# An earlier first product: one weight split traced behind two input tiles, and products of a zero tile during the first loads

## The chip, the cores and the metric

The kernel runs on one core of a Trainium2 chip. The metric is the device time of one execution in microseconds (us). The kernel before took 1235.92 us as the median of three runs (1230.69, 1235.92 and 2627.81 us).

## What is computed

Two layers of an encoder trunk over 512 tokens of width 1024, all in float32. Each layer normalises its input, projects it into the operands of an attention group (q, k, v) and of a bidirectional scan group (z, x/B/C, dt), joins both results in an output projection with a residual, and adds a gated feed-forward part. Cut to what matters here:

```python
for i in range(DEPTH):                      # DEPTH = 2
    h = rms_norm(x, norm_mix_w[i])
    proj = jnp.einsum("bld,de->ble", h, w_in[i])
    q, k, v, z, xbc_raw, dt_raw = jnp.split(proj, split_at, axis=-1)
    ...
    x = x + jnp.einsum("ble,ed->bld", mixed, w_out[i])
    h = rms_norm(x, norm_ffn_w[i])
    g = jnp.einsum("bld,df->blf", h, w_gate[i])
    u = jnp.einsum("bld,df->blf", h, w_up[i])
    x = x + jnp.einsum("blf,fd->bld", jax.nn.silu(g) * u, w_down[i])
return rms_norm(x, final_norm_w)
```

The change touches the first projection of layer 0 alone: the columns for k, v and dt (272 of them, "kvdt"), and what stands ahead of it.

## The kernel before

The activations are held transposed, as eight tiles x of 128 features by 512 tokens. Weights come in pieces of up to 1024 columns by 128 partitions. A product of two float32 operands is made from three products in TensorE's float32r format: each operand is split into a rounded high part and the rest, and high x high, high x low and low x high are added up in PSUM.

**Splitting.** W is a stream of weight pieces in a fixed order. W.split(j) (lines 180 to 195) takes piece j: ScalarE casts it to the high part whi (line 191), VectorE subtracts that from the raw piece and gives wlo (line 192). W.next() hands out the next piece and splits up to two ahead. Raw pieces lie in two buffers called wraw; a piece that is split frees its buffer, and the load of a later piece waits for that on the SP queue (line 177). The inputs are split in the same way: Norm.tile(k) casts x tile k times the norm's weights to xh on ScalarE (line 306) and computes xl on VectorE (line 307). Norm.square(k) squares a tile into one of two buffers sqt (line 319) and adds it to ssq (line 322).

**The start.** SP issues the loads of x tile 0, a small piece of the parameters (line 242), and x tiles 1 to 7 (line 240). ScalarE's queue issues pieces 0 and 1 of kvdt (piece 0 in two halves) and then pieces 2 and 3, which get a place of their own ("early"). The trace order is then: split of piece 0, split of piece 1, the eight tiles with the splits of pieces 2 and 3 among them, the squares.

**The first projection.** For each k-step (one x tile), four blocks of 128 tokens get three products of 272 columns each (lines 418 to 420), so 12 products a k-step and 96 in all. Piece 0 holds the weights of k-steps 0 and 1, piece 1 of 2 and 3, and so on. The results stay in four PSUM banks (two of tag "a", two of "s") until the norm's scale is known: the sum of squares is added over partitions by eight small products (line 328), VectorE computes the reciprocal root rtok (lines 284 to 290), and ScalarE scales the banks into kvd (line 464).

**What follows.** Attention (first product with V: line 717), the fill-in projections (q first, 256 columns each, lines 418 to 420 again; the x/B/C projections at lines 410 to 412) and the scan are traced as three generators in turns. The norm's scale is spread over tokens by a full float32 product with a tile of ones (line 343). The feed-forward part's first cast of summed operands is at line 1013.

**Order.** The program is traced in this order, and then a planner puts each engine's instructions in an order of its own, from a simulation of the timeline in which trace order gives the priority:

```python
with tile.TileContext(nc, schedule_with_timeline_sim=True) as tc:
```

So what is traced later can run earlier where its engine would be free. Each engine then executes its list strictly in the planned order.

Of the kernel before, what the change touches and what calls it, by code (L numbers as in the profile page):

```python
# [15 lines left out]
F32 = mybir.dt.float32  # L16
# [7 lines left out]
P = 128  # L24
# [17 lines left out]
OUTE, _, YE, HE, WE, RAE, MLE, DSE = "AVGVGVVG"  # L42
# [36 lines left out]
def tile_hybrid_encoder(ctx, tc, xt_d, par_d, rope_d, snw_d, w_kvdt, w_xbc, w_q, w_z, w_out, w_gate, w_up, w_down, out_d):  # L79
    nc = tc.nc  # L80
    V, A, G, T = nc.vector, nc.scalar, nc.gpsimd, nc.tensor
# [4 lines left out]
    nrm = ctx.enter_context(tc.tile_pool(name="nrm", bufs=1))  # L86
# [9 lines left out]
    def bank(tag):  # L96


        return psum.tile([P, S], F32, name=f"ps_{tag}", tag=tag)
# [107 lines left out]
    W = Stream()  # L207
# [49 lines left out]
    for name, op in (("lt", ALU.is_gt), ("le", ALU.is_ge)):  # L257
        m = const.tile([P, P], F32, name=f"m_{name}")
        G.affine_select(out=m, in_=ones, pattern=[[1, P]], compare_op=op, fill=0.0, base=0, channel_multiplier=-1)
        mask[name] = m  # L260
    for name, op in (("gt", ALU.is_gt), ("ge", ALU.is_ge)):
        m = const.tile([P, P], F32, name=f"m_{name}")
# [7 lines left out]
    inv = const.tile([P, 1], F32, name="inv")  # L270
    V.memset(inv, 1.0 / D)

    warm = const.tile([P, 1], F32, name="warm")
    A.activation(warm, inv, AF.Tanh)

# [160 lines left out]
    def mixer(l, norm, mx):  # L436
        op = norm.op
        if l == 0:
            early = mx.tile([P, 2, WU], F32, name="early", tag="qr")
            for j in (2, 3):  # L440
                W.raw[j] = early[:, j - 2]
                W.fetch(j, 0, chunks[j][1], A)
            W.split(0)
            W.split(1)
            for k in range(KT):
                norm.tile(k)
                if k in (3, 5):
                    W.split(k // 2 + 1)
            for k in range(KT):
                norm.square(k, V, V if k == 0 else None)  # L450
# [516 lines left out]
    for l in range(L):  # L967
        with tc.tile_pool(name=f"mx{l}", bufs=1) as mx:
            norm = mixer(l, norm, mx)
        with tc.tile_pool(name=f"ff{l}", bufs=1) as ff:  # L970
# [46 lines left out]
            for f in range(PLAIN):  # L1017
# [11 lines left out]
                if f == 0:  # L1029
                    with tc.high_priority():  # L1030
                        _, rb = norm.finish()
# [160 lines left out]
```

## Time and profile before

| | |
|---|---|
| median of three runs | 1235.92 us |
| the profiled execution's own time | 1231.69 us |
| its span in the trace | 1230.0 us |
| TensorE busy | 1198.6 us, 97% |
| VectorE busy | 902.4 us, 73% |
| ScalarE busy | 630.5 us, 51% |
| GpSimd busy | 157.8 us, 13% |
| first product on TensorE | 9.42 us |

PE is TensorE (PEld its weight loads), DVE VectorE, ACT ScalarE, POOL GpSimd, SP SyncE, whose queue issues most DMAs. L191 is line 191 of the kernel. A busy TensorE isn't necessarily one at its peak: the ends of its products are modelled, so the distance from one start to the next says more than a duration. Where a row merges several instructions (x2), its time runs from the first start to the last end, and neighbouring instructions of one engine overlap in the records by about 0.1 us.

### The profile page before, as it was taken

Reading aid. Unit: us, or ns where it says so; the run is one execution under the profiler, and the core shown is the slowest. Engines: PE = TensorE matmul, PEld = TensorE weight load, DVE = VectorE, ACT = ScalarE, POOL = GpSimd, SP = SyncE. Lnnn points to the kernel's source line nnn. Section 1 sums busy time; section 2 is a strip of 40 time slices with the busy share of each in tenths; the row PEclk is TensorE's granted clock in tenths of the full one; section 3 lists DMA queues with packets and bytes.
Section 4 is the critical chain, followed back from the end, with each engine's and each line's share of the span. In section 5 each row is a group of like instructions: output and inputs, shape, how many; then the busy total and the mean of one; then the engine's idle time right before and its main releaser. Section 6 shows DMA issues by size and latency. Waiting matters only on the chain.

```text
span 1230.0 us, 19740 instructions
## 1 busy us (share of the span) xinstructions
PE 1198.6 (97%) x7718; PEld 1059.6 (86%) x7718; DVE 902.4 (73%) x1475; ACT 630.5 (51%) x1203; POOL 157.8 (13%) x144
## 2 busy tenths in 40 slices
PE   6999999999999999999999999999999999999996
PEld 6788886687899899899898898777879989989985
DVE  6898976457887677677679977856698847847843
ACT  5678675244354254254465776744444623623544
POOL 0203433011100000000202144401020000000002
PEclk9999999999999999999999999999999999999998
DMA  6221212224243234231442111212243333333121
GB/s 224 73 73 48 66 37 68 69 69 142 89 126 120 65 120 126 64 104 39 126 147 91 69 35 61 87 35 69 77 146 112 105 110 95 102 114 95 35 72 75
DMA packets 47534, 110.04 MB, mean 89 GB/s; under 512 B 5425, under 2 KB 5937, under 8 KB 47441
## 3 DMA queue, kind: packets, MB, share of 16 engines
q1 hardware_dynamic: 46720, 107.68, 27.7%
q8 instruction: 60, 0.98, 0.3%
q10 hardware_dynamic: 720, 1.11, 0.3%
q14 instruction: 34, 0.27, 0.1%
HBM read 104.44 MB, written 4.33 MB: 88 GB/s over the span
## 4 chain that ended last, share of the span: by engine, by line
PE 86%; DVE 9%; ACT 2%; issue 1%; DMA 1%; POOL 0%; ACTq 0%; DVEq 0%; POOLq 0%
PE ps_a L1054 6%; PE ps_a L1053 6%; PE ps_a L1052 6%; PE ps_a L410 5%; PE ps_a L411 5%; PE ps_a L412 5%; PE ps_a L1099 3%; PE ps_a L1098 3%; PE ps_a L1100 3%; PE ps_s L1098 3%; PE ps_s L1099 3%; PE ps_s L1100 3%; PE ps_s L1054 3%; PE ps_s L1053 3%; PE ps_s L1052 3%; PE ps_t L717 3%
## 5 line engine op out<-in xcount | busy, mean ns | idle before, releaser
L191 ACT CAST whi<-wraw 128x512 fp32r<-128x512 f32 (+4 forms) x183 | 125.5, 714 | 217.7 <-PE ps_a L411 57.6
L191 ACT CAST whi<-sraw 128x1024 fp32r<-128x1024 f32 x126 | 131.6, 1050 | 141.2 <-DVE sraw L166 40.7
L192 DVE TENSOR_TENSOR wlo<-wraw,whi 128x512 fp32r<-128x512 f32 (+4 forms) x183 | 152.5, 845 | 59.5 <-ACT whi L191 58.4
L192 DVE TENSOR_TENSOR wlo<-sraw,whi 128x1024 fp32r<-128x1024 f32 x126 | 153.5, 1223 | 46.5 <-ACT whi L191 46.3
L410 PE MATMUL ps_a<-xh,whi 128*128 128x512 f32 x320 | 128.3, 405 | 5.5 <-ACT kvd L464 1.7
L411 PE MATMUL ps_a<-xl,whi 128*128 128x512 f32 x320 | 128.2, 402 | 0.0
L412 PE MATMUL ps_a<-xh,wlo 128*128 128x512 f32 x320 | 127.8, 399 | 0.0
L322 POOL TENSOR_TENSOR ssq<-ssq,sqt 128x512 f32<-128x512 f32 x17 | 25.2, 1481 | 671.1 <-ACT sqt L319 670.8
L166 DVE TENSOR_TENSOR sraw<-sraw 128x1024 f32<-128x1024 f32 x72 | 88.0, 1222 | 1.0
L418 PE MATMUL ps_a<-whi,xh 128*128 128x256 f32 (+1 forms) x256 | 74.6, 292 | 9.4 <-ACT xh L306 9.4
L1054 PE MATMUL ps_a<-ss,wlo 128*128 128x256 f32 x288 | 81.7, 284 | 0.0
L1052 PE MATMUL ps_a<-ss,whi 128*128 128x256 f32 x288 | 81.5, 283 | 0.0
L1053 PE MATMUL ps_a<-ss,whi 128*128 128x256 f32 x288 | 81.5, 283 | 0.0
L1054 PE MATMUL ps_a<-s,wlo 128*128 128x256 f32 x288 | 81.1, 283 | 0.0
L1053 PE MATMUL ps_a<-s,whi 128*128 128x256 f32 x288 | 81.1, 283 | 0.0
L410 PEld LDWEIGHTS ps_a<-xh,whi 128*128 128x128 f32 x320 | 61.6, 193 | 22.1 <-ACT s L1013 4.0
L1052 PE MATMUL ps_a<-s,whi 128*128 128x256 f32 x288 | 79.8, 283 | 0.0
L411 PEld LDWEIGHTS ps_a<-xl,whi 128*128 128x128 f32 x320 | 61.4, 192 | 15.5 <-DVE xl L94 1.5
L419 PE MATMUL ps_a<-wlo,xh 128*128 128x256 f32 (+1 forms) x256 | 74.2, 291 | 0.0
L412 PEld LDWEIGHTS ps_a<-xh,wlo 128*128 128x128 f32 x320 | 61.4, 192 | 14.7 <-issue 2.0
L420 PE MATMUL ps_a<-whi,xl 128*128 128x256 f32 (+1 forms) x256 | 72.5, 287 | 0.0
L1098 PE MATMUL ps_s<-hid,whi 128*128 128x512 f32 (+1 forms) x182 | 69.9, 384 | 0.0
(399 smaller groups left out, 3420.4 us busy)
## 6 DMA issues: line engine op xcount, KB each, us to landing
sraw<-in_w_gate SPq DMA_DIRECT2D x72, 256.0 KB, 5.6
sraw<-in_w_up SPq DMA_DIRECT2D x72, 256.0 KB, 4.2
wraw<-in_w_down SPq DMA_DIRECT2D x48, 384.0 KB, 3.5
wraw<-in_w_xbc SPq DMA_DIRECT2D x16, 512.0 KB, 3.3
wraw<-in_w_out SPq DMA_DIRECT2D x16, 512.0 KB, 4.2
wraw<-in_w_q SPq DMA_DIRECT2D x8, 512.0 KB, 3.3
wraw<-in_w_z SPq DMA_DIRECT2D x8, 512.0 KB, 3.4
wraw<-in_w_gate SPq DMA_DIRECT2D x8, 512.0 KB
```

What stands on the lines that cost most here:

```text
L166: V.tensor_tensor(q[to], q[to], q[by], ALU.add)
L191: A.copy(hi[:, u], raw[:, u])
L192: (G if lo_pool else V).tensor_tensor(lo[:, u], raw[:, u], hi[:, u].bitcast(F32), ALU.subtract)
L410: T.matmul(ps, lhsT=wh, rhs=op.h[k], start=first, stop=False)
L411: T.matmul(ps, lhsT=wh, rhs=op.l[k], start=False, stop=False)
L412: T.matmul(ps, lhsT=wl, rhs=op.h[k], start=False, stop=last)
L418: T.matmul(ps, lhsT=xh, rhs=wh, start=first, stop=False)
L419: T.matmul(ps, lhsT=xh, rhs=wl, start=False, stop=False)
L1052: T.matmul(out, lhsT=wh[:, o:o + P], rhs=x_[:, 0, i], start=first and i + j == 0, stop=False, skip_group_check=True)
L1053: T.matmul(out, lhsT=wh[:, o:o + P], rhs=x_[:, 1, i], start=False, stop=False, skip_group_check=True)
L1054: T.matmul(out, lhsT=wl[:, o:o + P], rhs=x_[:, 0, i], start=False, stop=i == 3, skip_group_check=True)
L1098: T.matmul(ps[:, cols], lhsT=w1[:, o:o + P], rhs=h, start=f == a, stop=False)
```

## The change

A tile of zeros, 128 x 256, is set on VectorE, in one of the two buffers of the squares (tag sqt), and five full float32 products of it with itself are written into a bank of tag "m" that nothing reads. They are traced ahead of everything else that TensorE does. The split of weight piece 1 is no longer traced directly behind that of piece 0, but behind the first two input tiles; the splits of pieces 2 and 3 stay behind tiles 3 and 5.

```diff
@@ -270,6 +270,12 @@
     inv = const.tile([P, 1], F32, name="inv")
     V.memset(inv, 1.0 / D)
 
+
+    idle = nrm.tile([P, 256], F32, name="idle", tag="sqt", bufs=2)
+    V.memset(idle, 0.0)
+    b = bank("m")
+    for _ in range(5):
+        T.matmul(b[:, :256], lhsT=idle[:, :P], rhs=idle, start=True, stop=True)
     warm = const.tile([P, 1], F32, name="warm")
     A.activation(warm, inv, AF.Tanh)
 
@@ -441,10 +447,9 @@
                 W.raw[j] = early[:, j - 2]
                 W.fetch(j, 0, chunks[j][1], A)
             W.split(0)
-            W.split(1)
             for k in range(KT):
                 norm.tile(k)
-                if k in (3, 5):
+                if k in (1, 3, 5):
                     W.split(k // 2 + 1)
             for k in range(KT):
                 norm.square(k, V, V if k == 0 else None)
```

## Rows read from the trace of the kernel before

**Rows 1.** The page, part 1: busy time (share), instructions of each engine.
```profile
PE 1198.6 (97%) x7718; PEld 1059.6 (86%) x7718; DVE 902.4 (73%) x1475; ACT 630.5 (51%) x1203; POOL 157.8 (13%) x144
```

**Rows 2.** Timeline, first 10 us: start, length (us), engine, line, operation [idle before].
```profile
1.72 6.70 SPq L240 DMA_DIRECT2D x<-in_xt  x7
...
3.94 0.69 DVE L315 TENSOR_TENSOR ssq<-x 128x512 f32<-128x512 f32 x1 [2.95 <-DMA x<-in_xt]
4.32 0.74 ACT L191 CAST whi<-wraw 128x272 fp32r<-128x272 f32 x2 [0.61 <-DMA wraw<-in_w_kvdt]
...
8.10 0.64 ACT L191 CAST whi<-wraw 128x544 fp32r<-128x544 f32 x1 [3.04 <-DMA wraw<-in_w_kvdt]
...
8.65 1.33 ACT L306 ACTIVATE xh<-x,par 128x512 fp32r<-128x512 f32 x2
8.78 0.73 DVE L192 TENSOR_TENSOR wlo<-wraw,whi 128x544 fp32r<-128x544 f32 x1 [3.22 <-ACT whi L191]
...
9.42 1.41 DVE L307 SCALAR_TENSOR_TENSOR xl<-x,par,xh 128x512 fp32r<-128x512 f32 x2
...
9.42 0.59 PE L418 MATMUL ps_a<-whi,xh 128*128 128x272 f32 x1 [9.42 <-ACT xh L306]
```

**Rows 3.** Windows, TensorE: from:to, length, busy (instructions), granted clock, DMA share, GB/s.
```profile
9.40:14.80 5.40, 5.38 (x24) 1.00 1.01 377
14.80:24.12 9.32, 9.32 (x74) 1.00 0.34 111
32.60:35.40 2.80, 2.80 (x7) 0.50 0.01 3
```

**Rows 4.** Windows, all engines in order PE, PEld, DVE, ACT, POOL; clock, DMA.
```profile
10.00:15.00 5.00, 5.00 (x24) 5.00 (x23) 5.00 (x9) 5.00 (x10) 0.00 (x0) 1.00 1.01 376
```

**Rows 5.** Timeline, 28 to 33 us: sum of squares, kvd, first product of line 410.
```profile
28.68 0.95 PE L328 MATMUL ps_m<-inv,ssq 128*128 128x1 f32 x8
...
32.05 0.87 ACT L464 ACTIVATE kvd<-ps_a,rtok 128x272 f32<-128x272 f32 x2 [4.45 <-DVE rtok L290]
...
32.59 0.80 PE L410 MATMUL ps_a<-xh,whi 128*128 128x512 f32 x1 [1.66 <-ACT kvd L464]
```

**Rows 6.** Windows, all engines, as rows 4: a stretch ahead of the attention.
```profile
75.00:100.00 25.00, 25.00 (x156) 21.43 (x155) 24.76 (x46) 19.86 (x45) 0.00 (x0) 1.00 0.20 64
```

**Rows 7.** Lines 464, 717, 1013 by layer: ns min/median/max, first and last start.
```profile
L464 ACT ACTIVATE kvd<-ps_a,rtok x2: 481/484/488, 32.0 to 32.4; 128x272 f32<-128x272 f32 x2
L464 ACT ACTIVATE kvd<-ps_a,rtok x2: 482/485/488, 633.0 to 633.4; 128x272 f32<-128x272 f32 x2
L717 PE MATMUL ps_t<-t_ring,Vt x256: 272/273/324, 95.3 to 230.6; 128*64 128x128 f32 x128
L717 PE MATMUL ps_t<-t_ring,Vt x256: 272/273/324, 696.3 to 829.8; 128*64 128x128 f32 x128
L1013 ACT CAST s<-xn x3: 1039/1044/1058, 293.0 to 296.6; 128x1024 fp32r<-128x1024 f32 x3
L1013 ACT CAST s<-xn x3: 1040/1045/1058, 890.6 to 894.2; 128x1024 fp32r<-128x1024 f32 x3
```

**Rows 8.** The first parameter piece (tile par): its DMA from issue to landing.
```profile
DMA to landing us min/median/max: 3.1/3.1/3.1
```

**Rows 9.** Timeline, 20 to 26 us: both q pieces and the last squares.
```profile
20.21 0.33 SPq L177 DMA_DIRECT2D wraw<-in_w_q  x1
...
21.71 1.29 DVE L192 TENSOR_TENSOR wlo<-wraw,whi 128x512 fp32r<-128x512 f32 x2
...
23.64 1.14 ACT L191 CAST whi<-wraw 128x512 fp32r<-128x512 f32 x2 [1.18 <-DMA wraw<-in_w_q]
...
24.90 0.69 DVE L322 TENSOR_TENSOR ssq<-ssq,sqt 128x512 f32<-128x512 f32 x1
25.50 0.69 DVE L192 TENSOR_TENSOR wlo<-wraw,whi 128x512 fp32r<-128x512 f32 x1
```

**Rows 10.** Line 343, full float32 products of both layers: ns min/median/max, starts.
```profile
L343 PE MATMUL ps_m<-dg,ones x8: 591/592/592, 38.4 to 884.9; 128*128 128x512 f32 x8
```

## The prediction

> **What bounds the kernel now.** I read the page first, then the order of instructions in the first 45 us, then busy time by stretch, then single lines in both layers.
>
> The page has TensorE busy for 97% of the span [rows 1], so only stretches in which it is idle, or runs slowly, can give anything. The start is such a stretch. The timeline shows why [rows 2]: ScalarE finishes the cast of weight piece 0 at 5.06 us, then stands idle 3.04 us until the DMA of piece 1 lands at 8.10. The first two input casts (xh, line 306) are queued behind that cast, although the first input tile was there at 3.94, when VectorE squared it. They run at 8.65, VectorE has nothing to do from 5.56 to 8.78 in consequence, and the first product starts at 9.42.
>
> From there TensorE is dense but slow at first: 24 products in the 5.40 us to 14.80, then 74 in 9.32 us [rows 3]. That is 0.225 and 0.126 us each; for 272 columns these are 1.2 and 2.4 GHz. (The clock column has 1.00 in both; I go by the spacing.) The reader should now look at the feeders: from 10 us VectorE and ScalarE are busy in all of the 5.00 us, and the DMA share is 1.01 [rows 4]. So the front has two limits close together, TensorE and the engines that split its operands.
>
> The next wait is at 30.9 us. A product of line 410 needs a bank that ScalarE empties with kvd (line 464), which waits 4.45 us for rtok; that chain of VectorE starts behind the sum of squares, line 328, at 28.68; line 410 starts at 32.59 [rows 5]. After it VectorE is the bound up to the attention: 24.76 busy of 25 us between 75 and 100 [rows 6]. The time from kvd to the first attention product of line 717 is the same in both layers, 63.3 us [rows 7]. So the number to forecast is how much earlier **kvd** starts.
>
> **The change, part by part.**
>
> *The moved split.* It consists of one cast on ScalarE and one subtraction on VectorE; piece 1's DMA is issued earlier in the program, and its place is not changed. But the buffer of piece 1 is released by the subtraction, and the load of a q weight waits on SP for that release. The cast can't start before 8.10 in either kernel, so if both input tiles are through by then, this costs nothing. New on ScalarE: input cast 0 at 5.06, cast 1 at about 5.7, both done near 6.4 (1.33 us for two [rows 2]); on VectorE two subtractions (1.41 us) in the hole from 5.56 to 8.78. The first product moves from 9.42 to about 5.06 + 0.77 = 5.83 us (0.77 is from the start of the first cast, 8.65, to the product, 9.42): 3.6 us earlier. Needed are the parameters, which land 3.1 us after an issue that precedes 1.72, so by 4.8 [rows 2, 8], and tile 1. Its landing is not shown: its issue is at 1.72 and the second cast ran unhindered behind the first, by 9.3, so it lies between 4.8 (3.1 us, as the parameters) and 9.3. I take 5 to 6, nearer to the parameters and to tile 0, which was issued just ahead of it and was there at 3.94.
>
> *What this is worth behind 8.1 us.* ScalarE's list from there is shorter by two casts, 1.33 us, VectorE's by 1.41 us. If a square (0.6 us) and its addition (0.69) also slip into the hole, it is up to 1.9 and 2.1; if tile 1 lands at 9.3, nothing. As both engines are full in this stretch, what they produce comes earlier by that much, not by 3.6. I take 1.4. What TensorE needs from them last is the second q piece: its DMA is issued at 20.21, behind the release of a buffer, lands at 23.64, and its last subtraction ends at 26.19; the sum of squares is complete at 24.90 + 0.69 = 25.59 [rows 9]. With 1.4 taken off these are 24.8 and 24.2.
>
> *The sum of squares.* In the kernel before, 2.5 us of q products lie on TensorE between the last subtraction (26.19) and line 328 (28.68). TensorE came late there; now it would not. If all of them depend on that last piece, line 328 comes at 24.8 + 2.5 = 27.3, a gain of 1.4; if none do, at about 24.8, a gain of 3.9; with 2.1 in place of 1.4, at most 4.6. Half of the products take weights that were there before, so I take the middle, **2.6 us**, and keep 1.4 and 4.6. kvd starts 3.4 us behind line 328 as now, at 29.4.
>
> *The zero products.* One set of zeros on VectorE, idle before 3.94, and five products of 256 columns in full float32. The nearest row is line 343, 512 columns: eight records for the four norms, so two a product, 0.591 us each [rows 10]. As upper bound at half the clock I take the same 0.591 for 256 columns: 5 x 2 x 0.591 = 5.9 us, from about 1.2 to 7.1, which would hold up the first product by 1.3; as lower bound half of it, over by 4.2. Either way line 328 isn't touched, since k-steps 0 and 1 have to be done only by 9.4, when piece 1 is split. The tile takes one of two buffers of the squares until then; the squares of the first tiles that need the second come later. Cost **0**, between 0 and 0.6 (one square that misses the hole).
>
> What the clock is worth: if the products raise it, the 24 slow ones save 24 x (0.225 - 0.126) = 2.4 us of TensorE. But without that they would run from 5.83 to 11.2 and the other 72 to 20.3; the first q piece is subtracted at 21.71 to 23.00 [rows 9], now 1.4 earlier, at 20.3. TensorE would only wait there sooner. So the clock is worth **0** in my sum. The Trainium skill, "TensorE: Matmul & The Clock Gate" (Part 1: The HAM clock gate), says that the array starts at the low clock and that its own activity lifts it; this trace agrees about the rise. By that rule alone one would book the 2.4, and with the 3.6 the sum would be 1225.7.
>
> *Sum.* The profiled execution took 1231.69 us, 1.69 around its span; the median of the three runs is 1235.92, 4.2 above it, the fastest 1230.69. 1231.69 - 2.6 = **1229.1 us**.
>
> **The rivals.**
>
> *TensorE alone sets the front.* The feeders' idle hole is 3.2 us long, and if their lists can be pulled into it whole and the q weights come as early, the gain is 3.6 + 2.4 = 6.0: **1225.7**. For it: TensorE has no idle time between 9.42 and 30.9. Against it: VectorE and ScalarE have none either from 10 to 15 [rows 4]. Chance 0.2.
>
> *Nothing changes.* The instruction order is planned by a timeline simulation. If that puts piece 1's cast ahead of the input casts all the same, or if tile 1 lands near 9.3, the lists behind 8.1 are as long as before: **1231.7**. Chance 0.12.
>
> *The clock falls again.* If TensorE runs ahead and stands idle before the q products, they restart slow. The wait of 1.66 us at 32.59 [rows 5] was followed by 2.80 us at a granted clock of 0.50, that is 1.2 GHz [rows 3]; half of that is lost, 1.4 us, ahead of line 328: 1231.69 - 2.6 + 1.4 = **1230.5**. [...] Chance 0.13.
>
> *Slower: another order in layer 0's mixer.* An earlier front makes the planner interleave attention, scan and projections differently between kvd and the feed-forward. The price is seen in two orders of the same work: from kvd to the first cast of line 1013 layer 0 takes 293.0 - 32.0 = 261.0 us, layer 1 890.6 - 633.0 = 257.6 [rows 7]. A worse order by the same 3.4 gives 1231.69 - 2.6 + 3.4 = **1232.5**, and with the front's lower bound of 1.4, 1233.7. It decides once it costs more than the front gains. Layer 0 already has the longer of the two, which speaks against it. Chance 0.15.
>
> **How the numbers follow.** My forecast has 0.40. Low end: 1231.69 - 4.6 - 3.4 (a better order) = 1223.7, which takes in 1225.7. High end: 1233.7 and 3 us of the 4.2 by which the median lies above the profiled execution, about 1237. A difference of 2% is 24.7 us, about what a measurement can tell here; no case comes near. I leave 0.01 for faster, 0.02 for slower, where a planner's order could surprise, and 0.97 between.
>
> **What would show it.** Right: the first real product at 5.5 to 6.5 us; xh twice ahead of the cast of 128x544; that cast still at about 8.1; line 328 at 25 to 27.5; kvd at 28.5 to 31; 63 us from kvd to line 717. The zero products are right if they end before 7.1, and their use is seen in the spacing of the first 24. Wrong: a first product near 9.4 (the planner), kvd before 28 (TensorE alone), or a kvd that comes earlier while line 1013 does not (the order).

## The result: 0.9% faster, most of it 200 us behind the change

The changed kernel took **1223.53 us** (median of six runs, 1221.91 to 1226.36), the kernel before 1235.1 us (median of six, 1230.04 to 2627.81). The ratio is **0.9909 [0.9881, 0.9937]**; the execution of 2627.81 us is left out of it. The profiled execution took 1221.91 us with a span of 1219.8 us, against 1231.69 and 1230.0: 10.2 us less of span, where 2.6 had been forecast.

Lines of the changed kernel are 6 higher up to the first projection (L328 is now L334), and 5 higher from kvd on (L464 is L469, L717 is L722, L1013 is L1018). Of the page, part 1, as in [rows 1]:

```profile
PE 1194.8 (98%) x7728; PEld 1057.5 (87%) x7728; DVE 905.6 (74%) x1476; ACT 630.7 (52%) x1203; POOL 157.1 (13%) x144
```

The start of the changed kernel on the timeline, as in [rows 2]; then its sum of squares, kvd and first product behind it, as in [rows 5]:

```profile
1.28 4.12 PE L278 MATMUL ps_m<-idle 128*128 128x256 f32 x10 [1.28 <-DVE raw L596]
...
5.05 1.57 ACT L312 ACTIVATE xh<-x,par 128x512 fp32r<-128x512 f32 x2
...
5.82 0.39 PE L424 MATMUL ps_a<-whi,xh 128*128 128x272 f32 x1 [0.42 <-ACT xh L312]
...
7.16 0.65 ACT L191 CAST whi<-wraw 128x544 fp32r<-128x544 f32 x1 [0.53 <-DMA wraw<-in_w_kvdt]
...
22.92 0.95 PE L334 MATMUL ps_m<-inv,ssq 128*128 128x1 f32 x8
...
25.91 1.29 DVE L192 TENSOR_TENSOR wlo<-wraw,whi 128x512 fp32r<-128x512 f32 x2 [1.42 <-ACT whi L191]
...
27.12 0.15 DVE L336 TENSOR_SCALAR ms<-ps_m 128x4 f32<-128x4 f32 x1
...
29.48 0.87 ACT L469 ACTIVATE kvd<-ps_a,rtok 128x272 f32<-128x272 f32 x2 [3.09 <-DVE rtok L296]
...
30.03 0.50 PE L416 MATMUL ps_a<-xh,whi 128*128 128x512 f32 x1 [3.18 <-ACT kvd L469]
```

The zero products are over at 5.40, the first real product comes 3.6 us earlier, line 334 5.8 us earlier than line 328 did, and kvd 2.5 us earlier. The rest appears only later. The three landmarks of both layers, as in [rows 7]:

```profile
L469 ACT ACTIVATE kvd<-ps_a,rtok x2: 481/485/489, 29.5 to 29.9; 128x272 f32<-128x272 f32 x2
L469 ACT ACTIVATE kvd<-ps_a,rtok x2: 482/486/489, 622.1 to 622.5; 128x272 f32<-128x272 f32 x2
...
L722 PE MATMUL ps_t<-t_ring,Vt x256: 272/273/324, 99.0 to 208.8; 128*64 128x128 f32 x128
L722 PE MATMUL ps_t<-t_ring,Vt x256: 272/273/324, 686.1 to 819.4; 128*64 128x128 f32 x128
...
L1018 ACT CAST s<-xn x3: 1039/1044/1058, 282.8 to 286.4; 128x1024 fp32r<-128x1024 f32 x3
L1018 ACT CAST s<-xn x3: 1040/1045/1058, 880.2 to 883.8; 128x1024 fp32r<-128x1024 f32 x3
```

From kvd to the first cast of the feed-forward part layer 0 took 293.0 - 32.0 = 261.0 us before and takes 282.8 - 29.5 = 253.3 now. From there on nothing differs: cast to cast of the two layers 597.6 and 597.4, and from the second cast to the end 339.4 and 339.6. So the 10.2 us are **2.5 ahead of kvd and 7.7 between kvd and the feed-forward part of layer 0**, a stretch in which the change has not touched an instruction. The attention there even starts later (99.0 against 95.3), but ends 22 us earlier (208.8 against 230.6).

What is different in that stretch is the order of TensorE's list. The second half of the output projection (96 products of lines 410 to 412, now 416 to 418) needs only the scan; the normalisation of the attention (transposes of line 684, products of line 689, now 689 and 694, with ScalarE and VectorE between them) is a chain in which TensorE has little to do itself. Where do the 96 stand against it? Windows of the kernel before up to the first transpose, one each for the products of lines 410, 411 and 412 (length, busy, count; clock and DMA as in [rows 3]):

```profile
205.00:229.26 24.26, 9.43 (x24) 1.00 0.14 44
...
205.00:229.26 24.26, 9.50 (x24) 1.00 0.14 44
...
205.00:229.26 24.26, 9.29 (x24) 1.00 0.14 44
```

Its timeline: the first transposes and the chain's last products.

```profile
229.26 0.60 PE L684 MATMUL ps_t<-ident,rec 128*8 128x128 f32 x4
...
240.12 1.89 PE L689 MATMUL ps_s<-p_ring 8*128 8x512 f32 x2
```

The same window of the changed kernel, for line 416 (417 and 418 have none there), and its timeline:

```profile
205.00:207.42 2.42, 0.57 (x2) 1.00 0.01 3
```

```profile
207.42 0.60 PE L689 MATMUL ps_t<-ident,rec 128*8 128x128 f32 x4
...
219.04 1.98 PE L694 MATMUL ps_s<-p_ring 8*128 8x512 f32 x4
```

Before, 72 of the 96 are spent ahead of the chain and 24 are left to cover it; now 2 are spent, 34 lie within it and 60 behind it. Windows of TensorE (length, busy, granted clock) before: the stretch from kvd to the first cast, 10 us at its start, and the end of the chain:

```profile
32.05:293.00 260.95, 256.68 (x1550) 0.98 0.20 64
...
30.00:40.00 10.00, 8.34 (x33) 0.83 0.11 42
...
225.00:250.00 25.00, 24.89 (x93) 0.86 0.19 64
...
240.00:245.00 5.00, 5.00 (x10) 0.53 0.31 105
245.00:250.00 5.00, 4.89 (x17) 0.78 0.00 0
```

and in the changed kernel:

```profile
29.48:282.80 253.32, 249.75 (x1551) 1.00 0.20 66
...
225.00:250.00 25.00, 25.00 (x112) 1.00 0.29 96
```

Before, TensorE runs out of cover, and its granted clock falls to 0.53 in one window and 0.78 in the next: (1 - 0.53) x 5 + (1 - 0.78) x 5 = 3.45 us of full clock are lost. Another (1 - 0.83) x 10 = 1.7 are lost right behind kvd, where [rows 3] has a granted clock of 0.50. Now the clock stays at 1.00 in the whole stretch. TensorE's idle time in it falls from 4.27 to 3.57 us, another 0.7. Together these are 5.85 of the 7.7, at most, since a microsecond of lost clock need not cost a whole one; the rest I could not assign to rows.

### The profile page after: what moved, and what is told of

Its sections match the earlier page's. It is cut to its first block, busy times and chain, and to the rows that moved or that the text cites. A ratio compares the mean times of both kernels' runs of the same rounds, so it can differ in the third digit from the quotient of the medians.

```text
span 1219.8 us, 19780 instructions
## 1 busy us (share of the span) xinstructions
PE 1194.8 (98%) x7728; PEld 1057.5 (87%) x7728; DVE 905.6 (74%) x1476; ACT 630.7 (52%) x1203; POOL 157.1 (13%) x144
## 4 chain that ended last, share of the span: by engine, by line
PE 89%; DVE 6%; ACT 2%; DMA 1%; issue 1%; POOL 0%; ACTq 0%; DVEq 0%; POOLq 0%
PE ps_a L1059 6%; PE ps_a L1058 6%; PE ps_a L1057 6%; PE ps_a L416 5%; PE ps_a L417 5%; PE ps_a L418 5%; PE ps_a L1103 3%; PE ps_s L1103 3%; PE ps_a L1104 3%; PE ps_a L1105 3%; PE ps_s L1104 3%; PE ps_s L1105 3%; PE ps_t L722 3%; PE ps_s L1059 3%; PE ps_s L1058 3%; PE ps_s L1057 3%
## 5 line engine op out<-in xcount | busy, mean ns | idle before, releaser
L192 DVE TENSOR_TENSOR wlo<-wraw,whi 128x512 fp32r<-128x512 f32 (+4 forms) x183 | 149.4, 828 | 58.5 <-ACT whi L191 57.4
L328 POOL TENSOR_TENSOR ssq<-ssq,sqt 128x512 f32<-128x512 f32 x17 | 25.0, 1473 | 667.7 <-ACT sqt L325 667.5
```

Of the source, the lines that this page charges most:

```text
L192: (G if lo_pool else V).tensor_tensor(lo[:, u], raw[:, u], hi[:, u].bitcast(F32), ALU.subtract)
```

## The experiments

**Theory A**: the moved split makes the planner order layer 0's mixer otherwise, and that order is worth 7 to 8 us, whatever moves it there; the front gives 0.5 to 2.5. **Rival B**: the zero products and the clock of the first products give the time. All times from kvd (us) and the ratios stand in one table at the end of this section; "ahead" is how many of the 96 products each kernel's planned list for TensorE has ahead of the normalisation, by layer (the traces show the same for all of them).

**split_only**: the moved split alone.

```diff
-    idle = nrm.tile([P, 256], F32, name="idle", tag="sqt", bufs=2)
-    V.memset(idle, 0.0)
-    b = bank("m")
-    for _ in range(5):
-        T.matmul(b[:, :256], lhsT=idle[:, :P], rhs=idle, start=True, stop=True)
```

> The split of weight piece 1 moved, no zero products. Theory A (the moved split gives the time: 2.6 us at kvd, because the feeders' work starts in the hole before 8 us, and 7.7 us between kvd and the first cast of the feed-forward, because the planner now puts the attention of layer 0 ahead of its first output half): first real product at 5.8 us, the first 24 products spaced by 0.225 us, kvd at 28.5 to 30 us, kvd to first cast 253 us, a time 8 to 11 us under the kernel before. Rival B (the zero products carry it, by the clock): kvd hardly earlier than 31, less than 4 us under the kernel before.

1222.64 us, 0.9905 [0.9871, 0.9939]: all of the change's gain without its zero products. The rows show that these raise the clock, as B says, and that it buys nothing. Without them the first 24 products start at 6.24 and need 5.40 us (window of TensorE in split_only):

```profile
6.20:11.60 5.40, 5.36 (x24) 1.00 1.03 368
```

In the changed kernel 24 take 3.10 us, 0.129 each, which is the higher clock:

```profile
5.80:8.90 3.10, 3.08 (x24) 1.00 1.03 386
```

But kvd comes at 29.48 there and at 29.73 here, so the 2.30 us are not passed on. Two rows of split_only's timeline:

```profile
7.56 0.72 ACT L306 ACTIVATE xh<-x,par 128x512 fp32r<-128x512 f32 x1 [1.38 <-DMA x<-in_xt]
...
29.73 0.87 ACT L463 ACTIVATE kvd<-ps_a,rtok 128x272 f32<-128x272 f32 x2 [2.62 <-DVE rtok L290]
```

The second input tile landed for a cast at 7.56 only, which delays what TensorE needs next at either clock. (The landing belongs to this execution; a comparison without it is both_no_zeros below.)

**zero_only**: the zero products alone.

```diff
             W.split(0)
+            W.split(1)
...
-                if k in (1, 3, 5):
+                if k in (3, 5):
```

> The five zero products, the split of piece 1 left where it was. Theory A: first real product at 9.4 us as before; the time within 2 us of the kernel before, since the planned order of layer 0 is the old one (72 of the 96 products of the first output half ahead of line 684's transposes); kvd at 31 to 32; kvd to first cast 261 us. Rival B (clock): the first 24 products at 0.126 us from 9.4 on, kvd 2 to 3 us earlier, and 3 us or more under the kernel before. Open in both: whether the clock has fallen again by 9.4.

1231.78 us, 0.9986 [0.9962, 1.0011]: nothing, and the order stays that of before (262.4 us from kvd to the cast). For the clock alone this is a weak test, since the first products started slow here as well (window 9.40 to 14.80 in the last section). B falls by split_only, which has all of the gain without the zero products.

**old_front_new_order**: the kernel before, with eight settings of unused tiles (128 x 512) on VectorE, traced ahead of layer 0's attention, which only disturb the planner (the part up to `else` in the edit never applies).

```diff
+        if l == 0:
+            for _ in range(8):
+                V.memset(cwh[:, 40:41] if False else mx.tile([P, 512], F32, name='dum', tag='gg', bufs=GGB), 0.0)
         Vt = mx.tile([P, NC, P], F32, name="Vt")
```

> The kernel before, front untouched, with eight clears of an unused 128x512 tile on VectorE ahead of the copy of Vt in layer 0; with them the planner gives layer 0 the new order (2 of 96 products ahead of line 684). The clears cost at most 8 x 0.53 = 4.3 us where VectorE is full. Theory A (the order of the mixer is worth 7.7 us by itself): kvd at 32 as before, kvd to first cast 253 us plus 0 to 4.3, 3.4 to 7.7 us under the kernel before. Rival C (the gain behind kvd comes from the earlier front, the order only goes with it): kvd to first cast 261 us or more, a time equal to or above the kernel before.

1225.6 us, 0.9932 [0.9906, 0.9958]. The front is that of before; the planner now puts 2 products ahead of the chain, and the stretch shortens by 7.1 us. The settings themselves ran at the start of the program, not in the stretch (line 541; line 464 in layer 0; the cast on the timeline):

```profile
L541 DVE MEMSET dum<- x8: 485/485/485, 1.1 to 6.5; 128x512 f32 x8
...
L464 ACT ACTIVATE kvd<-ps_a,rtok x2: 480/484/488, 31.6 to 32.0; 128x272 f32<-128x272 f32 x2
```

```profile
285.49 1.05 ACT L1016 CAST s<-xn 128x1024 fp32r<-128x1024 f32 x1 [1.56 <-DVE xn L1009]
```

So the order gives the time without any of the change in the kernel. That is A's main claim.

**new_front_old_order**: the changed kernel with twelve such settings, which bring the order of before back (72 ahead).

```diff
+        if l == 0:
+            for _ in range(12):
+                V.memset(mx.tile([P, 512], F32, name='dum', tag='gg', bufs=GGB), 0.0)
```

> The changed kernel with twelve clears of an unused 128x512 tile on VectorE ahead of the copy of Vt in layer 0; with them the planner gives layer 0 the old order again (72 of 96). The clears cost at most 12 x 0.53 = 6.4 us. Theory A: kvd at 29.5 as in the changed kernel, kvd to first cast 261 us plus 0 to 6.4, so between 2.6 us under and 4 us over the kernel before. Rival C (the earlier front carries the gain): kvd to first cast 253 us plus 0 to 6.4, 4 to 10 us under the kernel before.

1232.25 us, 1.0003 [0.9979, 1.0028]; kvd to cast 292.7 - 31.8 = 260.9, as before, and the clock falls again at the same place (window of TensorE):

```profile
240.00:245.00 5.00, 5.00 (x10) 0.50 0.33 105
```

As a price of the new front alone it failed, since kvd came at 31.8: the planner also rearranged the first projection, and it put the settings among the first splits on VectorE:

```profile
L546 DVE MEMSET dum<- x12: 485/485/485, 1.3 to 10.4; 128x512 f32 x12
```

It shows only that with the old order the gain behind kvd is gone.

**layer1_order**: layer 1 still has 72 ahead. Giving the small operations of the norm's scale priority, in both layers, makes the planner take the order with 2 there as well.

```diff
-        norm.scales()
+        with tc.high_priority():
+            norm.scales()
```

> The changed kernel with the sum of squares of both layers planned at high priority. Layer 0 keeps its order; in layer 1 the planner now also puts 2 (not 72) of the 96 products of the first output half ahead of line 684's transposes. Nothing else is changed. Theory A (this order is what the 7.7 us came from): kvd in layer 0 at 29.5 as in the changed kernel; in layer 1 kvd to first cast of the feed-forward 250 to 254 us in place of 258, so 1216 to 1220 us, 4 to 8 us under the changed kernel. Rival C (the order goes with the gain without making it, the early start of layer 0 does): layer 1 keeps 258 us, the time stays within 1 us of the changed kernel.

1220.39 us, 0.989 [0.9857, 0.9922]. My expectation for kvd to cast in layer 1 missed: 258.2 us, not shorter. But layer 1's attention now starts 53.8 us behind kvd instead of 64.0, TensorE gets a new hole there, and no longer has a slow stretch behind it (windows of TensorE):

```profile
725.00:750.00 25.00, 23.45 (x163) 1.00 0.16 54
825.00:850.00 25.00, 25.00 (x112) 1.00 0.30 104
```

In the changed kernel:

```profile
725.00:750.00 25.00, 25.00 (x185) 1.00 0.21 65
825.00:850.00 25.00, 24.67 (x91) 0.93 0.19 63
```

From cast to cast it is 594.0 against 597.4: worth 3.4 us in layer 1, not 7.7. These 3.4 us lie ahead of layer 1's kvd, which comes 335.8 us behind layer 0's cast instead of 339.3; so this run doesn't tell the order from the priority itself. In layer 0 kvd came at 31.5, not at the 29.5 expected.

**layer1_between**: the same aim by the turns of the three generators in layer 1.

```diff
+        NA, NF_, NS = (1, 2, 3) if l == 0 else (2, 4, 5)
         drain((att(), NA), (fill(), NF_), (ssd(), NS))
```

> The changed kernel with the three generators of layer 1 traced in turns of 2, 4 and 5 steps in place of 1, 2 and 3; the planner then puts 36 of the 96 products ahead of line 684's transposes in layer 1, between 72 and 2, and 36 more inside the normalisation. Theory A (what counts is how many products are left to cover the normalisation): with 36 under it instead of 24 the granted clock stays at 1.00 through it and layer 1's kvd to first cast falls to between 252 and 257 us, 1 to 6 us under the changed kernel. Rival C: 258 us as before.

1219.94 us, 0.9893 [0.9866, 0.9919]. It puts 36 products ahead, 36 within and 24 behind. The clock stays up (the same window), the attention starts as in the changed kernel, and cast to cast is 594.4:

```profile
825.00:850.00 25.00, 25.00 (x112) 1.00 0.27 87
```

Here the gain lies behind layer 1's kvd (254.9 us to the cast instead of 258.1), where the order is what differs. Two quite different orders, nearly one result. What they share is that the chain is covered to its end and the clock doesn't fall.

**sum_first**: in the changed kernel the sum of squares is done at 23.9, but VectorE first runs two subtractions of an x/B/C piece (the row at 25.91), which wait for their cast, and only then takes ms (27.12). Here they are held behind the norm's scale.

```diff
-                V.tensor_scalar(dg[:, c * P:(c + 1) * P], ident, rt[:, c:c + 1], None, ALU.mult)
+                self.last = V.tensor_scalar(dg[:, c * P:(c + 1) * P], ident, rt[:, c:c + 1], None, ALU.mult)
...
-                    (G if lo_pool else V).tensor_tensor(lo[:, u], raw[:, u], hi[:, u].bitcast(F32), ALU.subtract)
+                    with tc.issue_after(nrm0.last.ins) if j == 7 else nullcontext():
+                        (G if lo_pool else V).tensor_tensor(lo[:, u], raw[:, u], hi[:, u].bitcast(F32), ALU.subtract)
```

> The changed kernel with the low part of the sixth streamed weight behind piece 5 (the second x/B/C piece) made to wait on VectorE's list for the norm's scale, so that the sum of squares, which is ready at 23.9 us, is not held up until 27.12 by two subtractions that wait for a DMA. Theory A (kvd is held by the order on VectorE, not by TensorE): kvd at 26.5 to 27.2 in place of 29.5, layer 0's mixer behind it unchanged at 253 us, so 2 to 3 us under the changed kernel. Rival D (the feeders or the weights bound the stretch behind kvd anyway): kvd earlier, but the first attention product no earlier than 98 to 99 us, and the time within 1 us of the changed kernel.

1220.98 us, 0.9899 [0.9872, 0.9925]. The timeline has what the edit is for:

```profile
23.26 0.95 PE L335 MATMUL ps_m<-inv,ssq 128*128 128x1 f32 x8
...
24.57 0.15 DVE L337 TENSOR_SCALAR ms<-ps_m 128x4 f32<-128x4 f32 x1
...
26.93 0.87 ACT L470 ACTIVATE kvd<-ps_a,rtok 128x272 f32<-128x272 f32 x2 [0.34 <-DVE rtok L297]
...
27.87 1.29 DVE L193 TENSOR_TENSOR wlo<-wraw,whi 128x512 fp32r<-128x512 f32 x2
```

kvd comes 2.6 us earlier, and so does the cast (280.2). Against the changed kernel the intervals of the whole overlap, so by the time alone this isn't shown; cast to cast it lost 1.7 us of the 2.6 again, where the clock fell further in layer 1 (below).

**both**: layer1_order and sum_first together.

> The changed kernel with both edits: the sum of squares ahead of the second x/B/C piece on VectorE in layer 0, and the high priority that gives layer 1 the new order. Theory A: the gains add, 6 to 11 us under the changed kernel, 1213 to 1218 us. Rivals C and D: no more than 1 us under the changed kernel.

1216.96 us, 0.9868 [0.9842, 0.9893], within the 1213 to 1218 of theory A.

**changed_again**: the changed kernel itself, on the chip of the next two.

> The changed kernel once more, beside the next two on the same chip. Open is how much of the 2.6 us at kvd depends on when input tile 1 lands: where the second xh cast waits for it until 7 us or later, kvd should come at 30 to 31.5 and not at 29.5, and the time 1 to 2 us later. Expected 1221.5 to 1226 us, 7 to 11 us under the kernel before.

1224.27 us, 0.9935 [0.9912, 0.9959]. kvd at 30.2 instead of 29.5, by other landing times, and the stretch behind it 254.9: the clock fell behind kvd, as in the kernel before.

**both_no_zeros**: both, without the zero tile and its products.

> The version with both edits (sum of squares ahead of the second x/B/C piece, high priority in both layers), the moved split kept, the five zero products and their tile left out. Planned order in both layers as with them (2 of 96). Theory A (feeders bound the front, the clock gives nothing there): within 2 us of the version with the zeros, so 1215 to 1219 us, kvd at 27 to 28.5. Rival B (the raised clock counts once the list on VectorE is in order): kvd 1.5 to 3 us later than with the zeros (27.2), 1218.5 to 1220 us.

**1215.28 us, 0.9859 [0.9837, 0.9882]**, the best kernel of the study: 1.4% faster than the one before; the interval of changed_again, beside which it ran, lies wholly above its own. The zero products are not missed:

```profile
26.59 0.86 ACT L465 ACTIVATE kvd<-ps_a,rtok 128x272 f32<-128x272 f32 x2 [0.34 <-DVE rtok L291]
```

**both_between**: sum_first with layer1_between.

> The changed kernel with the sum of squares ahead of the second x/B/C piece, and layer 1's generators in turns of 2, 4, 5 in place of high priority. Both parts were worth something apart: about 2.5 us at kvd, and 3.0 us in layer 1. If they add: 1216 to 1219 us, kvd at 27, layer 1 kvd to first cast 255 us. If layer 1's part depends on how layer 0 is planned, 1220 to 1222 us.

1216.61 us, 0.9871 [0.9848, 0.9893], as both.

| kernel | ahead, layers 0, 1 | kvd | kvd to cast, layer 0 | cast to cast | ratio |
|---|---|---|---|---|---|
| before | 72, 72 | 32.0 | 261.0 | 597.6 | 1 |
| zero_only | 72, 72 | 31.0 | 262.4 | 599.1 | 0.9986 [0.9962, 1.0011] |
| new_front_old_order | 72, 72 | 31.8 | 260.9 | 597.7 | 1.0003 [0.9979, 1.0028] |
| changed | 2, 72 | 29.5 | 253.3 | 597.4 | 0.9909 [0.9881, 0.9937] |
| changed_again | 2, 72 | 30.2 | 254.9 | 599.0 | 0.9935 [0.9912, 0.9959] |
| split_only | 2, 72 | 29.7 | 253.3 | 597.5 | 0.9905 [0.9871, 0.9939] |
| old_front_new_order | 2, 72 | 31.6 | 253.9 | 599.1 | 0.9932 [0.9906, 0.9958] |
| sum_first | 2, 72 | 26.9 | 253.3 | 599.1 | 0.9899 [0.9872, 0.9925] |
| layer1_order | 2, 2 | 31.5 | 254.8 | 594.0 | 0.9890 [0.9857, 0.9922] |
| both | 2, 2 | 27.2 | 253.9 | 595.1 | 0.9868 [0.9842, 0.9893] |
| both_no_zeros | 2, 2 | 26.6 | 253.2 | 594.0 | 0.9859 [0.9837, 0.9882] |
| layer1_between | 2, 36 | 30.4 | 253.2 | 594.4 | 0.9893 [0.9866, 0.9919] |
| both_between | 2, 36 | 27.2 | 253.2 | 594.4 | 0.9871 [0.9848, 0.9893] |

The fourth column has two groups and nothing between: 260.9 to 262.4 with 72 ahead in layer 0, 253.2 to 254.9 with 2. Neither the front nor the zero products move a kernel from one to the other.

What a fall of the clock costs with the order unchanged can be read in layer 1, where eight kernels have 72 ahead. Window of TensorE in changed_again, and at the start of layer 0's stretch:

```profile
825.00:850.00 25.00, 24.67 (x83) 0.86 0.14 45
...
30.00:40.00 10.00, 9.22 (x36) 0.83 0.05 21
```

In four of the eight (before, new_front_old_order, changed, split_only) the clock between 825 and 850 is 0.93, and cast to cast takes 597.4 to 597.7 us; in the other four it is 0.86, and it takes 599.0 to 599.1. So (0.93 - 0.86) x 25 = 1.75 us more of lost clock cost 1.5. Within the group of 2 in the fourth column it is the same: the two at 254.8 and 254.9 are those with 0.83 from 30 to 40, the others have 1.00 there. By this price the 5.15 us of clock that the kernel before lost are an estimated 4.4 of the 7.7, and about 1.5 of them, those behind kvd, are not the order's. With the same fall behind kvd on both sides the order of layer 0 is worth about 6 us (260.9 and 261.0 against 254.8 and 254.9).

## Why the prediction was right or wrong, point by point

The forecast was 1229.1 us, with a range from 1223.7 to about 1237 and nearly all chance within 2%. The time did stay within 2%; the median of 1223.53 lies 0.2 us below the low end. The profiled execution, from which the forecast was worked out, came 7.2 us below it (1221.91): the 2.5 at kvd were as forecast, by luck, as shown below, and the 7.7 behind it the forecast did not have.

- **First product, zero products.** Right: 5.82 (5.83 forecast), xh ahead of the cast of piece 1, zeros over at 5.40 (4.2 to 7.1) at no cost. That they raise the clock and gain nothing was right too; split_only shows it.
- **"The cast can't start before 8.10 in either kernel."** Wrong: it started at 7.16 here and at 8.37 in layer1_between. The landing is not a property of the kernel but varies by over a microsecond from execution to execution. Tile 1 was there for the cast behind xh of tile 0 in this trace, and first at 7.56 in split_only.
- **Line 328 at 26.1, kvd 3.4 behind it at 29.4.** kvd at 29.48 hit the number by two errors that cancel. Line 334 started at 22.92, 5.8 us earlier: the rival in which TensorE alone sets the front (gain 6.0) was right up to there. But the 3.4 us became 6.6, since VectorE's list had two subtractions that wait for a cast ahead of ms. I had taken the distance for a chain of work; it contains a place in a list, and what stood ahead in that list was not due to the same event. sum_first, which changes only that place, brings it to 3.7 (23.26 to 26.93).
- **"63.3 us in both layers, passed on 1:1."** Wrong: about 69.5 in every kernel with the new order (71.1 in the two whose clock fell behind kvd). This is the step that failed: I passed the gain at kvd on to the end unchanged, as if the list behind it stayed the same; instead the stretch from kvd to the cast shrank from 261.0 to 253.3. Nor did [rows 6] show VectorE as the bound up to the attention: TensorE is busy for all 25.00 us of that row.
- **The rival of another order in layer 0's mixer.** The mechanism was named and it happened, but with the other sign and twice the size: -7.7 us (about 1.5 of it the clock behind kvd) against the +3.4 of the forecast and the -3.4 of the range's low end. The price came from comparing layer 0 with layer 1 of the kernel before, as "two orders of the same work". Both have 72 products ahead: as to what matters here it was one order twice, and their difference was no bound for a third. Layer 0 had the longer stretch, which I did write down, as a word against a worse order; it spoke for a better one just as well.
- **"The clock falls again" ahead of the q products.** TensorE did wait there, for the low part of a q weight, and the clock stayed:

```profile
20.19 0.39 PE L425 MATMUL ps_t<-wlo,xh 128*128 128x256 f32 x1 [1.36 <-DVE wlo L192]
```

```profile
20.00:25.00 5.00, 4.81 (x40) 1.00 0.66 204
```

It also stayed behind the longer wait for kvd (3.18 us at 30.03, against the 1.66 of [rows 5]), but only in this execution; in changed_again, the same kernel, it fell there (0.83 from 30 to 40).

Where the clock cost most was at 240 us, in the kernel before, where I had not looked: the page's clock row has a 9 there, since a slice of it is 30.75 us long and the fall lies within 10.

Open: what makes up the other 3.3 of the 7.7 us that the lost clock doesn't explain; and why the order is worth about 6 us in layer 0 but 3.4 in layer 1 (cast to cast). The fall at 240 us is deeper than the one in layer 1 (3.45 us lost against 1.75), which explains about half of that difference. That the clock's fall is the largest part is an estimate from layer 1; no run kept the old order in layer 0 and held the clock up.

## What to carry to other kernels

Where a planner sets the order, an edit of two lines at the start can re-order a stage 200 us away, and that may be worth more than the edit. Before pricing such a change, list for the stages with a long chain between engines how much independent work the order leaves to cover it, and look for stretches with a lower granted clock in windows of 5 us; a rearrangement that could mend one is a term of its own, with a range from nothing to what the stretch loses. Where several executions have the same order and a different clock, they give the price of a fall. And take a distance such as "kvd comes 3.4 us behind the sum" apart into work and places in a list before moving one end of it.

## What the runs showed of the hardware

Idle time and the clock did not go together simply. TensorE waited 1.66 us in the kernel before, and its granted clock was 0.50 (the lower level, 1.2 GHz) in the 2.80 us that followed [rows 3]. In zero_only it waited as long at the same place, and the clock was 1.00 (2.4 GHz) in 2.80 us. The changed kernel waited 3.18 us and it was 1.00; the same kernel in changed_again waited 3.05 us, and it fell (0.83 from 30 to 40, shown above). First zero_only, then the wait of changed_again:

```profile
31.50 0.50 PE L416 MATMUL ps_a<-xh,whi 128*128 128x512 f32 x1 [1.65 <-ACT kvd L470]
```

```profile
31.50:34.30 2.80, 2.80 (x12) 1.00 0.02 6
```

```profile
30.78 0.50 PE L416 MATMUL ps_a<-xh,whi 128*128 128x512 f32 x1 [3.05 <-ACT kvd L469]
```

Nor do the eight products of one column decide it (line 328, 0.95 us): in the kernel before and in zero_only alike they ended 1.3 us ahead of the wait. So neither the length of the wait nor the list ahead of it told whether the clock would fall; what does stays open. In zero_only TensorE also waited 3.59 us behind the zero products, and the products after that started slow (timeline, then a window of TensorE):

```profile
9.47 0.59 PE L424 MATMUL ps_a<-whi,xh 128*128 128x272 f32 x1 [3.59 <-ACT xh L312]
```

```profile
9.40:14.80 5.40, 5.33 (x31) 0.71 1.03 382
```

The Trainium skill, "TensorE: Matmul & The Clock Gate" (HAM oscillation — how this bites in real kernels), has the clock go back by how long a gap is; here a gap of 1.66 us was followed by a fall and one of 3.18 was not.

Products whose operands are all zero count as activity: behind 4.12 us of them the first 24 real products took 3.10 us in the changed kernel, against 5.40 in split_only without them. They did not always lift the clock in time: in sum_first they took 4.63 us, up to 5.91, and the first products behind them, from 6.29 to 6.97, still started 0.23 us apart.
